# Pooling layer in groups of 1024 tokens, its input units as seven half-block products: a two-layer float32 trunk on one core

## The chip, the core and the metric

The kernel runs on one core of a Trainium2 chip. The core has five engines with a queue of instructions each: TensorE (PE, matrix products, into the banks of PSUM), VectorE (DVE), ScalarE (ACT), GpSimd (POOL) and SyncE (SP, which here issues all DMAs, in order). Each queue runs in its own order, and an instruction waits for semaphores of others. The metric is the device time of one execution in microseconds. Three runs of the kernel before gave 2665.26, 2665.99 and 2666.0 us, median 2665.99.

## What is computed

4096 tokens of width 1024 go through two layers with a norm ahead of each and one at the end, all in float32. The first layer is attention in a window of 128 with a learned sink for each head; the second subtracts each channel from its trailing mean over 2, 4, 8 or 16 tokens, mixes channels in four groups and gates the result.

```python
def attn_layer(h, w_in, sinks, w_out):
    proj = h @ w_in
    q, k, v, z = jnp.split(proj, ...)
    o = swa_with_sinks(q, k, v, sinks)
    return (o * jax.nn.silu(z)) @ w_out

def pool_layer(h, w_in, w_mix, scale, w_out):
    u, z = jnp.split(h @ w_in, [POOL_WIDTH], axis=-1)
    p = multiscale_pool(u)
    m = jnp.einsum('bsgc,gcd->bsgd', p, w_mix).reshape(B, S, POOL_WIDTH) * scale
    return (m * jax.nn.silu(z)) @ w_out

def reference(...):
    for i in range(DEPTH):
        h = rmsnorm(x, norm_g[i])
        y = attn_layer(...) if i % N_MIXERS == 0 else pool_layer(...)
        x = x + y.astype(x.dtype)
    return rmsnorm(x, final_g)
```

## The kernel before

Tokens are columns. They are worked on in 8 groups of 512 (`G`), first all groups through attention (s = 0 to 7), then all through pooling (s = 8 to 15). A **unit** is the product of 256 output channels with 512 tokens over all 1024 inputs: 48 matmuls (`in_piece`, L238). Every float32 operand is split into a high part, rounded to PE's float32r, and a low part that holds the rest (`split_sb`: ACT writes the high part, L121, DVE subtracts for the low part, L122); the three products high x high, high x low, low x high (`PASSES`) are accumulated. That gives 8 chunks of inputs x 2 halves of outputs x 3 passes.

An attention group has units k, v, q (4), z (4) and, for the group before it, four output units; between their matmuls stand 16 softmax items (4 sets of heads x 4 blocks of 128 queries): `it_scores` (scores, masked, exponentials on ACT), 0.9 of a unit later `it_turn` (transposes on PE, then DVE and POOL), 0.8 later `it_pv`. A pooling group has units u (4) and z (4), and four output units of the group before it. The pooling weights for u are first multiplied with the mixing matrices (`prep_load`, `prep_mm`, into `wum` in memory), so that mixing and input projection are one product.

The order of work is a list of events: `at(t, fn, ...)` notes what is to be done at time t, counted in units, with the offsets in the table `T`; the list is sorted by t and run once to build the program, and the framework then puts the instructions on each engine's queue by its own plan. In the last attention group (s = 7) z ends the group; the first pooling group (s = 8) goes u, z, u, then the four output units of s = 7, then the rest. So products of the pooling layer stand ahead of attention's last output units and behind them.

Weights are loaded and split when a unit first uses them (`w_load`, `w_split`), the parts are stored (`wparts`) and loaded again for later groups (`w_again`, 1024 KB at a time, L149, three tiles). The residual stream between the layers goes through memory: `x1` is written by `ev_o` (L456) and read by `xt_load` (L161) and `res_load`. Sums of squares for the norms are made in passing (`square`), summed over channels by a product with ones (`total`), sent through memory to be laid out differently (`rsd`, `rsq`) and broadcast (`spread`, L213). The last output unit is cut in two halves of 256 tokens, so that the end of the first half runs beside the second (`last_piece`, L473; `last_final`, L503).

Of the kernel before, what the change touches and what calls it, by code (L numbers as in the profile page):

```python
# [21 lines left out]
NG = S // G  # L22
NB = G // 128
# [14 lines left out]
         a2=6.8, a3=9.3, ad=0.55, pl=1.3, pm=0.5, pmd=0.5, aturn=0.9, apv=0.8)  # L38
# [7 lines left out]
def trunk_kernel(ctx, tc, xt, ng, w_a_in, sinks, w_a_out, wu_t, wmix, pscale, w_b_z, w_b_out, fg, out):  # L46
# [4 lines left out]
    hp = E(tc.tile_pool(name="hp", bufs=1))  # L51
    wp = E(tc.tile_pool(name="wp", bufs=1))
    sp = E(tc.tile_pool(name="sp", bufs=1))
    psum = E(tc.tile_pool(name="psum", bufs=1, space=PSUM))

    x1 = [dram.tile([4, 128, 2, G], F32, name=f"x1_{g}") for g in range(NG)]
    rsd = [dram.tile([1, G], F32, name=f"rsd_{g}") for g in range(3 * NG)]
# [20 lines left out]
    one8 = const.tile([128, 4, 128], I8, name="one8")  # L78
    nc.gpsimd.memset(one8, 1)
    mask = const.tile([128, 4, 128], I8, name="mask")  # L80
    nc.gpsimd.affine_select(out=mask, in_=one8, pattern=[[0, 4], [1, 128]], compare_op=ALU.is_ge,
                            fill=0.0, base=-1, channel_multiplier=-1)
    ucar = const.tile([128, 4, 2, 16], F32, name="ucar")
    nc.vector.memset(ucar, 0.0)
    cfix = const.tile([128, 4, 16], F32, name="cfix")
    nc.vector.memset(cfix, 1.0)
    for j, w in enumerate(WINDOWS):
        for t in range(w - 1):
            nc.gpsimd.memset(cfix[:, j, t:t + 1], float(w) / (t + 1))

# [12 lines left out]
    pool_tiles = {}  # L103
# [54 lines left out]
    def xt_load(s):  # L158
        for n in range(4):
            t = sp.tile([128, 2, G], F32, tag="xt", bufs=4, name=f"xt{s}_{n}")  # L160
            nc.sync.dma_start(t, xt[s, n] if s < NG else x1[s - NG][n])  # L161
            xts[s, n] = t
# [14 lines left out]
    def rstd(key, near=False):  # L177
# [7 lines left out]
        parts = [sp.tile([128, G], F32R, tag=t, bufs=1, name=f"{t}{key}") for t in ("sr", "sl")]  # L185
# [14 lines left out]
    def spread(key, near=False):  # L200
# [10 lines left out]
        nc.sync.dma_start(rsq[key].rearrange("o (p c) -> (o p) c", c=NB), rs)  # L211
        bc = sp.tile([128, G], F32, tag="bc", bufs=1, name=f"bc{key}")
# [6 lines left out]
    def x_scale(s, k):  # L219
        t = xts[s, k // 2][:, k % 2]  # L220
        nc.vector.scalar_tensor_tensor(t, t, ng_sb[:, s // NG, k:k + 1], bcs[s], op0=ALU.mult, op1=ALU.mult)  # L221
# [182 lines left out]
    us = {}  # L404

    def ev_u(U, s, j):
        ps = acc.pop(U)
        first = s == NG
        u = sp.tile([128, 2, G + 16], F32, tag="q", bufs=2, name=f"u{s}_{j}")
        nc.scalar.copy(u[:, :, 0:16], ucar[:, j])  # L410
        nc.scalar.copy(u[:, :, 16:], ps)  # L411
        nc.scalar.copy(ucar[:, j], u[:, :, G:G + 16])
        if "sums" not in pool_tiles:
            pool_tiles["sums"] = sp.tile([128, 2, 2, G + 16], F32, tag="vm", name="sums")
        tmps = [pool_tiles["sums"][:, i] for i in range(2)]
        w = WINDOWS[j]
        src, step, lo, i = u, 1, 0, 0
        while step < w:
            dst = tmps[i]
            lo += step  # L420
            nc.vector.tensor_add(dst[:, :, lo:], src[:, :, lo:], src[:, :, lo - step:G + 16 - step])
            src, step, i = dst, 2 * step, 1 - i
        if first:
            nc.vector.tensor_mul(src[:, :, 16:32], src[:, :, 16:32], cfix[:, j].unsqueeze(1).to_broadcast([128, 2, 16]))
        p = sp.tile([128, 2, G], F32, tag="o", bufs=2, name=f"p{s}_{j}")
        nc.vector.scalar_tensor_tensor(p, src[:, :, 16:], 1.0 / w, u[:, :, 16:], op0=ALU.mult, op1=ALU.subtract)
        us[s, j] = p

    def gate_b(s, j):
        gate(s, j, us.pop((s, j)))  # L430


    ress = {}
    rslot = [0]

    def res_load(s, n):
        if s < NG:
            t = sp.tile([128, 2, G], F32, tag="res", bufs=2, name=f"res{s}_{n}")
            nc.sync.dma_start(t, xt[s, n])
        else:  # L440
            i = rslot[0] % 5
            rslot[0] += 1
            if "res" not in pool_tiles:
                pool_tiles["res"] = sp.tile([128, 5, 2, G], F32, tag="kt", name="resb")
            t = pool_tiles["res"][:, i]
            nc.sync.dma_start(t, x1[s - NG][n])
        ress[s, n] = t

    def ev_o(U, s, n):
        ps = acc.pop(U)  # L450
        t = ress[s, n]
        if s == 2 * NG - 1 and n == 3:
            return
        nc.vector.tensor_add(t, t, ps)  # L454
        if s < NG:
            nc.sync.dma_start(x1[s][n], t)  # L456
            del ress[s, n]
            return
        square(NG + s, n, t, nc.vector)


    HT = G // 2

    def last_piece(U, i8):
        s, half = 2 * NG - 1, i8 // 4
        cols = slice(HT * half, HT * half + HT)
        if i8 % 4 == 0:
            acc[U] = mm_tile(f"mm{U}_{half}")
        ps = acc[U]
        for k in range(2 * (i8 % 4), 2 * (i8 % 4) + 2):  # L470
            for c in range(2):
# [35 lines left out]
    def final(s):  # L507
        bc = bcs.pop(NG + s)
        for k in range(NK):
            t = ress[s, k // 2][:, k % 2]  # L510
            nc.vector.scalar_tensor_tensor(t, t, fg_sb[:, k:k + 1], bc, op0=ALU.mult, op1=ALU.mult)
            if k % 2:
                nc.sync.dma_start(out[s - NG, k // 2], ress.pop((s, k // 2)))
# [200 lines left out]
```

## Time and profile before

| | |
|---|---|
| median of three runs | 2665.99 us |
| the profiled execution | 2667.01 us, of which the span is 2665.3 |
| mean granted clock of PE | 0.997 of full speed |
| matmuls of units, 128x512, with h (L238) | 6528, 1549.2 us busy |
| matmuls of output units, 128x512, with a (L238) | 3024, 703.3 us busy |
| matmuls of scores (L331) | 1024, 148.6 us busy |
| memory traffic | 487.65 MB read, 92.36 MB written, 218 GB/s over the span |

The profile lists busy time by engine and by group of instructions (line, engine, operation, tiles out<-in, shapes, count; busy us, mean ns of one; idle time of the engine just before them and what ended it). It also gives busy time in any stretch of time, who waited for whom, and instructions in order of time. PE is matmuls, PEld the weight loads beside them. A group's mean is of single durations; matmuls overlap, so their rate is read from start to start.

### The profile page before, as it was taken

How to read it: one execution, taken by the hardware profiler on the slowest of the kernel's cores; microseconds unless marked ns; L12 is line 12 of the kernel's file. 1: busy time of each engine (PE TensorE's matmuls, PEld its weight loads, DVE VectorE, ACT ScalarE, POOL GpSimd, SP SyncE). 2: the span in 40 equal slices, each digit the busy share in tenths (PEclk: the TensorE clock that was granted, in tenths of full speed). 3: DMA queues.
4: the chain of work that ended last, by engine and by line, in shares of the span. 5: the costliest groups of instructions: out<-in, count | busy, mean ns of one | idle time of the engine just before them, and what ended most of it. 6: DMA issues, size and time to landing. Idle time of an engine off the chain costs nothing.

```text
span 2665.3 us, 34728 instructions
## 1 busy us (share of the span) xinstructions
PE 2602.9 (98%) x12732; PEld 2185.8 (82%) x12732; DVE 1611.1 (60%) x2744; ACT 993.4 (37%) x2528; POOL 629.6 (24%) x984
## 2 busy tenths in 40 slices
PE   6999999999999999999999999999999999999998
PEld 5878888888888888888888878888888888888887
DVE  6898667576576675675685674554545454535343
ACT  5566345354354353353462442322222222222111
POOL 1353343343343352352443330000000000000000
PEclk9999999999999999999999999999999999999999
DMA  7855754655555555546546478876767676767564
GB/s 277 292 195 187 267 189 170 213 177 187 195 180 184 194 180 185 198 169 217 182 173 219 163 276 302 290 256 228 256 237 252 230 255 226 261 222 261 195 245 155
DMA packets 109814, 582.29 MB, mean 218 GB/s; under 512 B 18102, under 2 KB 20150, under 8 KB 56396
## 3 DMA queue, kind: packets, MB, share of 16 engines
q1 hardware_dynamic: 109644, 580.07, 61.9%
q8 instruction: 101, 1.65, 0.2%
q14 instruction: 69, 0.57, 0.1%
HBM read 487.65 MB, written 92.36 MB: 218 GB/s over the span
## 4 chain that ended last, share of the span: by engine, by line
issue 42%; PE 40%; DVE 11%; ACT 4%; DMA 2%; POOL 2%; POOLq 0%; SPq 0%; DVEq 0%; ACTq 0%
PE mm L238 29%; PE s L331 3%; PE mm L248 3%; ACT P L346 2%; PE pT L358 2%; PE po L389 1%; DVE m L369 1%; DVE m L365 1%; DVE h L122 1%; POOL rs L204 1%; DVE xt L221 1%; DVE sq L173 1%; DVE mx L342 1%; DVE o L398 1%; DVE q L283 1%
## 5 line engine op out<-in xcount | busy, mean ns | idle before, releaser
L238 PE MATMUL mm<-h,w 128*128 128x512 f32 x6528 | 1549.2, 392 | 7.1 <-DMA w<-wparts 3.8
L238 PEld LDWEIGHTS mm<-h,w 128*128 128x128 f32 x6528 | 1207.1, 188 | 249.8 <-DMA w<-wparts 5.9
L238 PE MATMUL mm<-a,w 128*128 128x512 f32 x3024 | 703.3, 390 | 0.6 <-ACT u L411 0.6
L238 PEld LDWEIGHTS mm<-a,w 128*128 128x128 f32 x3024 | 563.4, 188 | 115.6 <-ACT u L411 1.1
L346 ACT ACTIVATE P<-s,nm 128x128 f32<-128x128 f32 x512 | 181.3, 367 | 266.5 <-DVE nm L343 216.4
L351 POOL TENSOR_TENSOR P<-P,sm 128x512 f32<-128x512 f32 x128 | 141.0, 1101 | 565.3 <-DVE sm L350 355.0
L204 POOL TENSOR_TENSOR rs<-ms,mhalf 128x4 f32<-128x4 f32 x23 | 26.4, 1150 | 1024.4 <-DVE ms L203 947.1
L377 POOL TENSOR_SCALAR_AFFINE_SELECT m<-m 64x512 fp32r<-64x512 f32 x256 | 189.2, 739 | 59.0 <-DVE m L369 55.7
L314 DVE SCALAR_TENSOR_TENSOR sz<-th,mm 128x512 f32<-128x512 f32 x128 | 87.7, 685 | 146.2 <-ACT th L313 144.7
L375 POOL TENSOR_SCALAR_AFFINE_SELECT m<-m 64x256 fp32r<-64x256 f32 x256 | 117.0, 457 | 229.6 <-ACT m L364 221.2
L397 ACT COPY tmp<-po 64x256 f32<-64x256 f32 x256 | 94.1, 368 | 192.4 <-DVE o L398 95.1
L454 DVE TENSOR_TENSOR resb<-resb,mm 128x1024 f32<-128x1024 f32 x31 | 37.9, 1221 | 207.6 <-PE mm L238 207.6
L331 PEld LDWEIGHTS s<-kt,q 128*128 128x128 f32 x1024 | 141.1, 191 | 19.8 <-ACT P L346 4.8
L173 DVE TENSOR_TENSOR sq<-sq,sr 128x512 f32<-128x512 f32 x166 | 118.2, 712 | 64.4 <-ACT sr L172 62.6
L331 PE MATMUL s<-kt,q 128*128 128x256 f32 x1024 | 148.6, 285 | 4.1 <-ACT P L346 2.1
L313 ACT ACTIVATE th<-mm 128x512 f32<-128x512 f32 x128 | 76.6, 599 | 191.3 <-PE mm L238 142.6
L398 DVE TENSOR_TENSOR o<-po,tmp 64x256 f32<-64x256 f32 x256 | 108.0, 422 | 65.9 <-ACT tmp L397 60.5
L379 POOL TENSOR_SCALAR_AFFINE_SELECT m<-m 64x256 fp32r<-64x256 f32 x256 | 138.5, 541 | 13.6
L283 DVE TENSOR_TENSOR q<-mm,q 64x512 fp32r<-64x512 f32 x128 | 88.2, 689 | 61.2 <-ACT q L282 59.5
L337 DVE COPY_PREDICATED s<-mask,s 128x512 f32<-128x512 int8 x124 | 85.7, 691 | 57.8 <-PE s L331 57.0
L221 DVE SCALAR_TENSOR_TENSOR xt<-xt,ng_sb,bc 128x512 f32<-128x512 f32 x128 | 91.5, 761 | 41.2 <-DMA bc<-rsq 39.1
L172 ACT ACTIVATE sr<-resb 128x512 f32<-128x512 f32 x54 | 34.0, 629 | 216.2 <-DVE resb L454 198.4
(108 smaller groups left out, 2511.7 us busy)
## 6 DMA issues: line engine op xcount, KB each, us to landing
w<-wparts SPq DMA_DIRECT2D x364, 1024.0 KB, 4.9
wparts<-w SPq DMA_DIRECT2D x52, 1024.0 KB, 4.8
xt<-in_xt SPq DMA_DIRECT2D x32, 512.0 KB, 4.4
res<-in_xt SPq DMA_DIRECT2D x32, 512.0 KB, 3.4
x<-res SPq DMA_DIRECT2D x32, 512.0 KB, 5.9
xt<-x SPq DMA_DIRECT2D x32, 512.0 KB, 5.3
resb<-x SPq DMA_DIRECT2D x32, 512.0 KB, 5.2
out<-resb SPq DMA_DIRECT2D x28, 512.0 KB, 2.6
```

Source lines behind the costliest of these rows:

```text
L173: engine.tensor_add(sums[key], sums[key], q)
L221: nc.vector.scalar_tensor_tensor(t, t, ng_sb[:, s // NG, k:k + 1], bcs[s], op0=ALU.mult, op1=ALU.mult)
L238: nc.tensor.matmul(ps[:, c], w[:, wl, k % 4, 128 * c:128 * c + 128], rhs(k, hl), start=(k == 0 and i == 0), stop=(k == NK - 1 and i == 2))
L283: nc.vector.tensor_sub(q[64 - r:128 - r, h], src, f32(q[r:r + 64, h]))
L331: nc.tensor.matmul(ps[:, h], qs[s, j][:, h, 128 * b:128 * b + 128], kt[:, j, hl, 128 * b:128 * b + 256], start=(hl == 0), stop=(hl == 1))
L346: nc.scalar.activation(P[:, h], sc[:, h], AF.Exp, bias=nm[:, h:h + 1], scale=SCALE, accum_out=sm[:, h:h + 1])
L351: nc.gpsimd.tensor_mul(P, P, sm.unsqueeze(2).to_broadcast([128, 4, 128]))
L375: nc.gpsimd.affine_select(out=m2[own, :, cols], in_=f32(m1[own, 0, :, cols]), compare_op=ALU.is_ge, fill=0.0, **keep)
L377: nc.gpsimd.affine_select(out=mv, in_=f32(mv), compare_op=ALU.is_ge, fill=0.0, **drop)
L379: nc.gpsimd.affine_select(out=mv, in_=f32(mv), compare_op=ALU.is_ge, fill=0.0, **keep)
L397: nc.scalar.copy(tmp[d:d + 64], pv[e:e + 64, :, r])
L398: nc.vector.tensor_add(o[d:d + 64, :, 128 * b:128 * b + 128], pv[d:d + 64, :, r], tmp[d:d + 64])
```

## The change

**Groups and products.** Pooling now runs over four groups of 1024 tokens, two blocks of 512. An input unit (256 outputs x 1024 tokens over 1024 inputs) is seen as a product of 2x2 half-blocks: outputs in halves of 128, inputs in halves of 512, tokens in two blocks. The product of 2x2 blocks is formed with seven products in place of eight (`product`, L571), each of 12 matmuls, from sums of blocks (Winograd's form). The left factors, sums of weight blocks, are made once in attention groups 2 to 7: `seven_load` and `seven`, 24 calls, four to a group, with four POOL sums, seven splits and seven stores each for u and z, and four splits for output weights. The right factors, sums of blocks of tokens (T1 to T4 beside B11, B21, B22), are made for each group by POOL (`factor_sum`) and split by ACT and DVE (`factor`, L117 and L118). Seven products go into three PSUM banks X, Y, Z; as X is accumulated further for other results, its contents are copied out in between by ACT (`snapshot`), three times a unit. A unit's product 3 is done within the next unit.

**Order.** A pooling group runs its eight input units and then its own four output units (`o_pair`, L620, 96 matmuls each, four banks); pooling of one group and output of another no longer alternate. The pooling stage has its own pools of SBUF and PSUM, opened when attention's are closed (`open_pools`). The last attention group has another order of units and softmax offsets (`e0` to `e3`), and attention's last output units are followed by the pooling stage alone. The squares for the first pooling group's norm are made in attention (`x1_square`). The final norm of a group is applied in pieces during the next group (`final_piece`), from a copy in memory (`x2`); the last output unit is cut in pieces of 512, 256 and 256 tokens (`last_pair`, L741; `last_scale`, L783).

The core of the diff:

```diff
+NP = NG // 2
...
+        a11, a12, a21, a22 = v[:, 0, 0], v[:, 1, 0], v[:, 0, 1], v[:, 1, 1]
+        S = wp.tile([128, 4, 2, 128], F32, tag="wraw", bufs=2, name=f"sum7_{key[0]}{key[1]}_{hf}")
+        g = nc.gpsimd
+        g.tensor_add(S[:, 0], a21, a22)
+        g.tensor_sub(S[:, 1], S[:, 0], a11)
+        g.tensor_sub(S[:, 2], a11, a21)
+        g.tensor_sub(S[:, 3], a12, S[:, 1])
+        for i, m in enumerate((a11, a12, S[:, 3], a22, S[:, 0], S[:, 1], S[:, 2])):
+            t = sp.tile([128, 2, 2, 128], F32R, tag="sl", bufs=2, name=f"part7_{key[0]}{key[1]}_{hf}_{i}")
+            if i == 3:
+                nc.scalar.mul(t[:, 0], m, -1.0)
+                nc.vector.scalar_tensor_tensor(t[:, 1], m, -1.0, f32(t[:, 0]), op0=ALU.mult, op1=ALU.subtract)
+            else:
+                split_sb(t[:, 0], t[:, 1], m)
+            nc.sync.dma_start(wseven[key][i][:, hf], f32(t))
...
+    RIGHT = {1: "B11", 2: "B21", 3: "B22", 4: "T4", 5: "T1", 6: "T2", 7: "T3"}
...
+    def factor_sum(g, name, p):
+        ph = (g, "in")
+        b11, b12, b21, b22 = (quarter(ph, p, t, k) for k in range(2) for t in range(2))
+        sub = nc.gpsimd.tensor_sub
+        if name == "T1":
+            sub(b11, b12, b11)
+        elif name == "T3":
+            sub(b12, b22, b12)
+        elif name == "T2":
+            tmp2[p] = bt([128, G], "t2", 4, f"t2_{g}_{p}")
+            sub(tmp2[p], b22, b11)
+        else:
+            sub(tmp2[p], tmp2[p], b21)
...
+    def factor(ph, name, p):
+        src = quarter(ph, p, *PLACE[name]) if name in PLACE else tmp2[p]
+        t = bt([128, 2, G], "set", 28, f"set_{ph[0]}{ph[1]}_{name}_{p}", F32R)
+        split_sb(t[:, 0], t[:, 1], src)
+        sets[ph, name, p] = t
...
+    def w7_load(u, i):
+        src = wout[u[2]][i] if u[1] == "o" else wseven[u[1], u[2]][i - 1]
+        t = bt([128] + list(src.shape[1:]), "w7", 5, f"w7_{u[0][0]}{u[1]}{u[2]}_{i}", F32R)
+        nc.sync.dma_start(f32(t), src)
...
+    def product(u, i):
+        bank = {1: "X", 6: "X", 7: "X", 4: "X", 2: "Y", 5: "Z", 3: "Z"}[i]
+        first = i in (1, 2, 5)
+        if first:
+            banks[u, bank] = bpsum(bank, 2, f"{bank}_{u[0][0]}{u[1]}{u[2]}")
+        ps, w = banks[u, bank], w7.pop((u, i))
+        for a, p in enumerate(PAIRS):
+            t = sets[u[0], RIGHT[i], p]
+            for b, (wl, hl) in enumerate(PASSES):
+                nc.tensor.matmul(ps, w[:, p // 2, wl, p % 2], t[:, hl], start=(first and a == 0 and b == 0),
+                                 stop=(a == 3 and b == 2), skip_group_check=True)
...
+    def snapshot(u, n, t):
+        nc.scalar.copy(blk(u, n, t), banks[u, "X"])
...
+    def h_load(g, p):
+        r = raws[(g, "in"), p] = bt([128, 2, 2, G], "raw", 4, f"xr{g}_{p}")
+        for t in range(2):
+            nc.sync.dma_start(r[:, t], x1[2 * g + t][p])
...
+    def h_scale(g, p):
+        for k in range(2):
+            r = raws[(g, "in"), p][:, :, k]
+            nc.vector.scalar_tensor_tensor(r, r, ng_sb[:, 1, 2 * p + k:2 * p + k + 1], bbc["h", g], op0=ALU.mult, op1=ALU.mult)
...
+        if 2 <= s < NG:
+            for i in range(4):
+                k, hf = sevens[4 * (s - 2) + i]
+                t = base + 1.0 + 3.2 * i
+                at(t, seven_load, k, sources[k[0]][k[1]], hf)
+                at(t + 0.8, seven, k, hf)
...
+    at(base, open_pools)
...
+            order = [1, 6, 5, 7, 2, 4] if prev is None and g else [1, 2, 5, 6, 7, 4] if prev is None else [1, 3, 6, 5, 7, 2, 4]
```

**What moves on the engines.** SP's queue where attention ends, before the change (`x1_7` is the residual stream of the last attention group, `wum` and `in_w_b_z` are pooling weights):

```order
L456 DMA x1_7_79<-res7_2_15594 128x1024
L145 DMA wparts_115_0_15755<-w115_0_15752 128x2048
L136 DMA wraw116_0_15757<-wum_2_130 128x1024
L145 DMA wparts_115_1_15798<-w115_1_15795 128x2048
L136 DMA wraw116_1_15806<-wum_2_130 128x1024
L456 DMA x1_7_79<-res7_3_15651 128x1024
```

Weights of the next pooling units stand ahead of the last store of attention's results. The same place with the change (`w7_...` are left factors, `bch0` the norm's broadcast, `xr0_p` the activations of the first 1024 tokens, in four pairs of chunks p):

```order
L413 DMA x1_7_79<-res7_2_16134 128x1024
L413 DMA x1_7_79<-res7_3_16191 128x1024
L559 DMA w7_0u3_1_16367<-w7_u3_0_13078 128x1024
L559 DMA w7_0u3_2_16369<-w7_u3_1_13079 128x1024
L559 DMA w7_0u3_5_16371<-w7_u3_4_13082 128x1024
L559 DMA w7_0u3_6_16373<-w7_u3_5_13083 128x1024
L559 DMA w7_0u3_7_16375<-w7_u3_6_13084 128x1024
L703 DMA bch0_16377<-rsq_8_116 128x512
L703 DMA bch0_16377<-rsq_9_117 128x512
L708 DMA xr0_3_16380<-x1_0_72 128x1024
L708 DMA xr0_3_16380<-x1_1_73 128x1024
L708 DMA xr0_2_16383<-x1_0_72 128x1024
```

All loads of the pooling layer now stand behind that store, the weights first. PE's queue at the same place, before (`mm110` is the second u unit of the first pooling group, `mm111` the first output unit of attention's last group):

```order
L238 MATMUL mm110_15479<-h8_6_15163,w110_1_15438 128x512 x6
L238 MATMUL mm110_15479<-h8_7_15187,w110_1_15438 128x512 x6
L193 MATMUL ms9_15942<-sr9_15895,ones_r_144 128x512
L193 MATMUL ms9_15942<-sl9_15896,ones_r_144 128x512
L238 MATMUL mm111_15567<-a0_7_14509,w111_0_15486 128x512 x12
L238 MATMUL mm111_15567<-a1_7_14751,w111_0_15486 128x512 x12
```

And with the change (the last output unit of attention, then the first input unit `0u3`; `set_0in_B11_p` is a split right factor):

```order
L236 MATMUL mm111_16276<-a3_7_16104,w111_1_16254 128x512 x12
L571 MATMUL X_0u3_16482<-set_0in_B11_3_16394,w7_0u3_1_16367 128x512 x3
L571 MATMUL X_0u3_16482<-set_0in_B11_2_16400,w7_0u3_1_16367 128x512 x3
L571 MATMUL X_0u3_16482<-set_0in_B11_1_16406,w7_0u3_1_16367 128x512 x3
L571 MATMUL X_0u3_16482<-set_0in_B11_0_16412,w7_0u3_1_16367 128x512
L571 MATMUL Y_0u3_16498<-set_0in_B21_3_16416,w7_0u3_2_16369 128x512
```

The first pooling product comes directly behind attention's last matmul. ACT's queue in that first input unit (COPY rows of L588 are snapshots of bank X, CAST rows the high parts of factors); before the change there were no snapshots and no factors:

```order
L117 CAST set_0in_T3_0_16476<-xr0_0_16389 128x512
L588 COPY ct_0u3_16480<-X_0u3_16482 128x512
L117 CAST set_0in_T4_3_16529<-t2_0_3_16431 128x512
L117 CAST set_0in_T4_2_16532<-t2_0_2_16436 128x512
L117 CAST set_0in_T4_1_16535<-t2_0_1_16441 128x512
L117 CAST set_0in_T4_0_16538<-t2_0_0_16446 128x512
L117 CAST set_0in_B22_3_16555<-xr0_3_16380 128x512
L117 CAST set_0in_B22_2_16558<-xr0_2_16383 128x512
L117 CAST set_0in_B22_1_16561<-xr0_1_16386 128x512
L117 CAST set_0in_B22_0_16564<-xr0_0_16389 128x512
L588 COPY ct_0u3_16480<-X_0u3_16482 128x512
```

The unit's second snapshot stands behind the casts of T4 and B22.

531 lines of the change are left out of this document (387 added, 144 removed).

## The prediction

> **What bounds the kernel now.** I read the totals and the clock slices on the page first, then busy time in stretches of 200 us, then PE's waits, then the order in time where attention hands over to pooling.
>
> ```profile
> span 2665.3 us, 34728 instructions
> PE 2602.9 (98%) x12732; PEld 2185.8 (82%) x12732; DVE 1611.1 (60%) x2744; ACT 993.4 (37%) x2528; POOL 629.6 (24%) x984
> PEclk9999999999999999999999999999999999999999
> ```
>
> PE is busy 98% of the span at full clock. A busy PE alone proves little, so the stretches and the waits come next (columns: stretch, length, then busy us and instructions of PE, PEld, DVE, ACT, POOL, granted clock, DMA share, GB/s).
>
> ```profile
> 100.00:200.00 100.00, 95.14 (x485) 78.13 (x484) 89.10 (x168) 58.63 (x171) 51.67 (x77) 1.00 0.66 227
> 600.00:800.00 200.00, 197.32 (x1019) 167.19 (x1019) 135.36 (x273) 91.65 (x276) 81.11 (x127) 1.00 0.52 188
> 1800.00:2000.00 200.00, 200.00 (x884) 165.62 (x883) 91.26 (x109) 44.96 (x75) 2.39 (x2) 1.00 0.68 239
> PE mm L238 <- DMA w<-wparts: 3.8, 5, 1.3
> ```
>
> The last line is all that PE waited for between 1600 and 2620 us. Attention runs to about 1600 us, pooling from there. In both stages the matmul stream is the limit, and in pooling almost nothing interrupts it. The rate and the hand-over stand in PE's order in time:
>
> ```profile
> 1583.98 43.83 PE L238 MATMUL mm<-a,w 128*128 128x512 f32 x192 [0.65 <-ACT u L411]
> 1627.65 65.44 PE L238 MATMUL mm<-h,w 128*128 128x512 f32 x288
> 1692.93 27.36 PE L238 MATMUL mm<-a,w 128*128 128x512 f32 x120
> ```
>
> From start to start, (1692.93 - 1627.65)/288 = 0.2267 us for one matmul of 512 columns; 12 of them take 2.72 us. The hand-over costs 0.65 us today, because u and z products of the first pooling group stand on both sides of attention's last output units.
>
> **The change, part by part.** Sums are against the profiled run: 2667.01 us with a span of 2665.3, so 1.7 us lie around it; the median of the three runs is 1.0 lower. I apply the sum of changes to the median, 2665.99.
>
> *Matmuls, -87.0.* Pooling had 12 units x 8 groups x 48 = 4608 matmuls of 512 columns. Now four groups have 8 input units x 7 products x 12 = 672 and 4 output units x 96 = 384, together 4224 (the last output unit is in narrower pieces in both). 384 x 0.2267 = 87.0 us, and PE is what sets the end there, so all of it counts. Attention keeps its matmuls.
>
> *The hand-over, +44.* This is the large cost. The order on SP puts every load of the pooling layer behind the store of attention's last result. Nothing of PE's work is left to cover them, as attention's output units are now its last products. Rows for the walk (groups, then DMA issues with KB and us to landing, then two stretches of DMA):
>
> ```profile
> L122 DVE TENSOR_TENSOR h<-xt,h 128x512 fp32r<-128x512 f32 x128 | 90.4, 720 | 0.9
> L319 DVE SCALAR_TENSOR_TENSOR sz<-o,sz 128x1024 f32<-128x1024 f32 x32 | 39.1, 1221 | 0.5
> L454 DVE TENSOR_TENSOR res<-res,mm 128x1024 f32<-128x1024 f32 x32 | 39.1, 1222 | 48.5 <-PE mm L238 48.2
> L351 POOL TENSOR_TENSOR P<-P,sm 128x512 f32<-128x512 f32 x128 | 141.0, 1101 | 565.3 <-DVE sm L350 355.0 <-ACT m L364 81.0 <-PE mm L238 52.9
> L121 ACT CAST h<-xt 128x512 fp32r<-128x512 f32 x128 | 79.3, 620 | 54.1 <-PE mm L238 43.0 <-DVE xt L221 7.1 <-DVE h L122 1.5
> out<-resb SPq DMA_DIRECT2D x8, 256.0 KB, 2.5
> 204.00:206.00 2.00, 2.00 (x11) 1.61 (x10) 1.43 (x5) 1.95 (x8) 0.90 (x1) 1.00 0.96 385
> ```
>
> Clock zero is attention's last matmul. The residual add takes 1.2 us, the store's issue some 0.5. Ahead of the first activations' arrival lie the store (0.5 MiB), five weight tiles (2.5), two broadcasts (0.5) and those activations (1.0): 4.7 MB at 385 GB/s is 12.3 us. A 256 KB store takes 2.5 us to land, of which 0.7 is transfer, so 1.8 us is fixed. The first pair is there at about 15.9, the other three 2.7 apart.
>
> Then come scalings (8 at 1.22 on DVE) and splits into high part (ACT, 0.62) and low part (DVE, 0.72), while POOL makes the sums: 16 subtractions, priced like its 128x512 tensor_tensor at 1.10. If DVE and POOL overlapped, DVE alone would set the pace. These rows say they do not:
>
> ```profile
> 721.49 0.89 POOL L375 TENSOR_SCALAR_AFFINE_SELECT m<-m 64x256 fp32r<-64x256 f32 x2 [2.90 <-ACT m L364]
> 737.16 1.22 DVE L319 SCALAR_TENSOR_TENSOR sz<-o,sz 128x1024 f32<-128x1024 f32 x1
> 737.46 1.67 POOL L375 TENSOR_SCALAR_AFFINE_SELECT m<-m 64x256 fp32r<-64x256 f32 x2 [4.74 <-ACT m L364]
> ```
>
> The same two POOL selects take 0.89 us, but 1.67 when DVE is inside an operation with two SBUF operands: 737.46 + 1.67 - 0.89 = 738.24, about when DVE's operation ends (738.38). The scalings, the low parts and POOL's subtractions are all of that kind, so I add their times. (The Trainium skill, SBUF — State Buffer, section "Who interferes with whom", says the same: DVE's second SBUF input comes through the read interface that GpSimd uses, and the loser blocks for the whole instruction; this row agrees. Without that rule the sum would take the 29 us below for 45.)
>
> To POOL's last sum: 8 x 1.22 + 16 low parts x 0.72 + 16 x 1.10 = 38.9, so 54.8. ACT then casts that sum and, ahead of the second snapshot of bank X in its queue, four B22 factors: 5 x 0.62, and 0.62 for the snapshot, 58.5. Product 7 waits for it (61.2), product 4 for the next snapshot (with four other matmuls, about 64.9), product 3 ends at 67.6. PE has by then done 8 products and four matmuls, 22.7 us of work: **45 us idle**, 44 more than today. With DVE alone, POOL's last sum is at 15.9 + 21.3 + 1.1 = 38.3, and idle about 29. Worst, with 300 GB/s and both engines fully in series, 52.
>
> *Attention's added work, +13.* 24 calls of `seven` cut the pooling weights into parts: 112 subtractions of 256 columns and 32 of 512 on DVE, and 16 squares are made there too. By the nearest rows (0.42 for 256 columns, 0.72) that is some 80 us of DVE in groups 2 to 7, about 1200 us: its share goes from 0.68 to 0.75. In the two attention stretches above PE lost 1.3% at a DVE share of 0.68 and 4.9% at 0.89; in proportion, 0.067 more share costs 1.1% of 1200, 13 us. That includes the tighter last group. Below, nothing, if the spaces hide it; above, 4.9% throughout: 41.
>
> ```profile
> L478 DVE TENSOR_TENSOR resb<-resb,mm 128x256 f32<-128x256 f32 x4 | 1.5, 418 | 3.0 <-PE mm L473 3.0
> ```
>
> *Seams between pooling groups, +9.* At three seams the snapshot of a group's first product stands on ACT behind the squares of the old group's last output: after PE's last output matmul come an add (0.72), a square (0.62), POOL's add (1.10, behind two low parts, 1.4), a cast and the snapshot (0.62 each), 5.1 us, against 2.72 for the first product. So PE idles about 2.4 us, and then runs cold:
>
> ```profile
> 212.00:214.00 2.00, 1.23 (x6) 0.66 (x4) 2.00 (x5) 0.17 (x1) 0.00 (x0) 1.00 0.00 0
> 214.00:216.00 2.00, 0.79 (x2) 0.51 (x3) 1.19 (x4) 2.00 (x11) 0.00 (x0) 0.84 0.83 254
> 216.00:218.00 2.00, 2.00 (x10) 2.00 (x10) 0.98 (x3) 1.95 (x4) 1.04 (x1) 0.50 0.66 274
> 218.00:220.00 2.00, 2.00 (x10) 1.60 (x9) 1.85 (x4) 0.83 (x3) 0.00 (x0) 0.81 0.00 0
> 215.21 1.11 PE L238 MATMUL mm<-h,w 128*128 128x512 f32 x2 [1.98 <-DVE sz L314]
> ```
>
> A gap of 1.98 us left the granted clock at 0.84, 0.50 and 0.81 for 2 us each: 2 x (0.16 + 0.50 + 0.19) = 1.7 us lost. Three times 4.1 is 12.3, less the 3.8 us of weight waits, whose loads now have five tiles in flight. (The Trainium skill, TensorE: Matmul & The Clock Gate, "Part 1", wants an idle window of about 3.4 us before the clock halves; the row halves it after 1.98. By the page the seams would cost 3 x 2.4 - 3.8 = 3.) From 0 to 25 us: snapshots inside a unit have a whole product, 2.72 us, to be taken.
>
> *The tail, +4.*
>
> ```profile
> 2650.32 1.67 PE L473 MATMUL mm<-a,w 128*128 128x256 f32 x12
> 2658.74 3.22 DVE L503 SCALAR_TENSOR_TENSOR resb<-resb,fg_sb,bc 128x256 f32<-128x256 f32 x8 [2.09 <-PE bc L500]
> ```
>
> Today the last scaling begins 6.75 us after the last matmul (2651.99). Now the eight 512-wide scalings of the first 512 tokens, 8 x 0.72 = 5.8 us, stand in DVE's queue ahead of the last result, some 3 us of them past the last matmul, and the chain behind waits: about 4 us (0 to 6).
>
> *Memory traffic, 0.* A product takes one 512 KB tile per 2.72 us, 193 GB/s, today's rate for units; output units need half of that. With pieces of the last norm some 270 GB/s, under the 385 above. If that cover goes, each late tile costs what today's do, 0.8 us.
>
> Sum: -87.0 + 44 + 13 + 9 + 4 = -17; 2665.99 - 17 = **2649**.
>
> **Rivals.** *DVE and POOL overlap after all* (operands from PSUM do not block, and the sums might slip in between): hand-over 29 instead of 45, **2633**. For it: in the attention stretches DVE and POOL together are busy longer than the stretch; against it: most of DVE's operations there read PSUM, and the row above.
>
> *Slower: the parts' stores hold ACT and DVE.* `seven` has two slots for parts, so ACT's cast of a part waits in its queue until the store of two parts earlier has landed, with softmax work queued behind it.
>
> ```profile
> x<-res SPq DMA_DIRECT2D x32, 512.0 KB, 5.9
> PE pT L358 <- DVE m L369: 17.2, 11, 2.2
> ```
>
> A store in attention takes up to 5.9 us to land, an idle one 2.5. If each of the 24 calls made PE wait as long as its longest wait on DVE now, 2.2 us, that is 53 us, 40 above my 13: **2689**. It decides from (17 + 13)/24 = 1.25 us a call. Against it: the order spreads a call's parts among other rows on ACT, and the transposes stand 0.9 of a unit, about 10 us, after their scores.
>
> *Snapshots late inside the units*: 96 on ACT and each a possible gap. At 0.25 us each, 24 us: **2673**. Against it: ACT was 22% busy in pooling, and a product stands between.
>
> *The products are not as fast*: 12 matmuls now go to one bank in a row, where a unit's today change banks after 3. Each ns more is 4.2 us, so 4 ns would eat the gain: **2666**. No row shows such a price.
>
> **How the numbers follow.** Forecast as walked, 0.55: **2649**, with its terms' own spread from 2636 to 2665. Overlap or a cheaper hand-over, 0.25: 2608 to 2636. Slower by stores, 0.10; late snapshots, 0.07; slower products, 0.03: 2660 to 2700. The range takes in the first two and half of the rest: 2614 to 2676. A measurement here tells 0.2%, 5.3 us, from no change: faster means under 2660.7. From the forecast 0.48 lies below it and 0.07 within; with the second case, and 0.02 of the rest, faster is 0.75; within 0.12; slower 0.13.
>
> **What would show it.** PE's product rows should start 0.227 apart, with 4224 of them. Between attention's last matmul and pooling's steady run, PE should show about 45 us without work; if DVE's low parts there stay at 0.7 and POOL's subtractions at 1.1 while both are busy, the lock is wrong and 29 should stand. POOL's sums longer than 1.5 us would show it right. Waits of PE on DVE and ACT in attention should grow by 13 us in all. The three seams should show gaps of about 2 us with the clock at 0.50 behind. I am wrong if SP's loads start before attention's last store, or if PE's waits in groups 2 to 7 exceed 30 us.

## Result and the profile after

The changed kernel takes **2732.82 us** (median of 4 runs, 2728.4 to 2737.86) against 2665.99 (2665.26 to 2666.42): ratio 1.0252, 95% interval 1.0228 to 1.0275. It is 67 us slower, where 2649 was forecast in a range of 2614 to 2676. The profiled execution has a span of 2727.0 us, 61.7 more than before. First the totals and the clock slices of the page of after, then busy time in the two longer stretches shown of before, with the same columns:

```profile
span 2727.0 us, 35659 instructions
PE 2551.1 (94%) x12362; PEld 2124.1 (78%) x12362; DVE 1795.9 (66%) x2958; ACT 1076.8 (39%) x2774; POOL 871.2 (32%) x1164
PEclk9999999999999999999999997999899989998999
```

```profile
600.00:800.00 200.00, 195.63 (x996) 164.07 (x996) 147.86 (x299) 103.27 (x306) 88.31 (x130) 0.99 0.68 239
1800.00:2000.00 200.00, 176.54 (x767) 144.55 (x766) 128.71 (x139) 60.70 (x108) 54.11 (x34) 0.95 0.64 217
```

PE was busy 98% of the span and is busy 94%. The clock slices were 9 throughout and now have four dips: one where attention hands over, three later at equal distances. Attention lost a little, and the pooling stretch, which had no idle microsecond, has 23 us in 200. What PE waited for from 1600 us to the end (us in total, times, longest):

```profile
PE ms L684 <- ACT sro L117: 58.6, 3, 20.0
PE X_0u L571 <- ACT set_0in_B L117: 23.0, 4, 19.1
PE X_0u L571 <- DVE set_0in_B L118: 7.1, 4, 2.4
```

The hand-over is there as walked (X_0u: group 0). New is the first line: three waits of nearly 20 us in the norm total of the old group (`b_total`), one for each seam between pooling groups. PE's order in time gives the size of each term (start, us, then what; rows from attention's last matmuls to the last product):

```profile
1614.83 6.06 PE L236 MATMUL mm<-a,w 128*128 128x512 f32 x26
...
1905.10 2.88 PE L571 MATMUL X_1u<-set_1in_B,w_1u 128*128 128x512 f32 x12
1927.62 0.80 PE L684 MATMUL ms<-sro,ones_r 128*128 128x512 f32 x1 [19.64 <-ACT sro L117]
...
2056.26 2.88 PE L571 MATMUL X_1u<-set_1in_T,w_1u 128*128 128x512 f32 x12
2058.99 2.88 PE L571 MATMUL Y_1u<-set_1in_B,w_1u 128*128 128x512 f32 x12
...
2174.20 2.88 PE L571 MATMUL X_2u<-set_2in_B,w_2u 128*128 128x512 f32 x12
...
2441.27 2.88 PE L571 MATMUL X_3u<-set_3in_B,w_3u 128*128 128x512 f32 x12
...
2709.01 1.68 PE L741 MATMUL last<-set_3out_B,w_3o 128*128 128x256 f32 x12
```

A product starts 2.73 us after the one before it (2056.26, 2058.99): the cadence of 0.2267 us a matmul holds. A group has 672 + 384 matmuls and up to 8 of norm totals, 1064 x 0.2267 = 241.2 us. From start to start it takes 269.1 and 267.1, and 269.4 from the last start to the last matmul, where about 242 would do: **81 us lost in the three stretches that hold the seams**. Some 7 of them lie elsewhere: PE's short waits for snapshots inside the units (1.5 us at most). From attention's end (1620.9) to 1905.1 it is 284.2, where 240.3 would do (1060 matmuls): 43.9 for the hand-over. In before attention's last matmul ended at 1627.65 with 144 pooling matmuls done ahead of it by the order, so 32.6 us of that was pooling's; 1595.0 against 1620.9 is 26 for attention. From the last product to the end it was 13.3 and is 16.3. The division between two terms is this execution's: in nine later runs that left attention as it is, attention ended up to 10 us earlier, and in eight that left the hand-over as it is, that stretch was up to 6 us longer.

| term (us) | forecast | measured |
|---|---|---|
| matmuls | -87.0 | -87.0 |
| hand-over | +44 | +43 |
| attention | +13 | +26 |
| seams, less the weight waits of 3.8 | +9 | +77 |
| tail | +4 | +3 |
| sum | -17 | +62 (61.7 between the two spans) |

Now the first seam. DVE (1874 to 1927 us) and POOL (to 1928) from the first scaling of the next group on, grouped (count, busy us, mean ns, idle before), then PE, DVE and ACT in order of time where PE stands still:

```profile
L718 DVE SCALAR_TENSOR_TENSOR xr<-xr,ng_sb,bch 128x1024 f32<-128x1024 f32 x8 | 15.1, 1924 | 10.7 <-issue 10.7
L118 DVE TENSOR_TENSOR set_1in_B<-xr,set_1in_B 128x512 fp32r<-128x512 f32 x11 | 13.3, 1229 | 0.6 <-ACT set_1in_B L117 0.6
L118 DVE TENSOR_TENSOR set_1in_T<-xr,set_1in_T 128x512 fp32r<-128x512 f32 x8 | 13.0, 1687 | 0.0
```

```profile
L535 POOL TENSOR_TENSOR xr<-xr 128x512 f32<-128x512 f32 x4 | 8.5, 2137 | 10.6 <-DVE set_1in_B L118 10.6
L540 POOL TENSOR_TENSOR t<-xr 128x512 f32<-128x512 f32 x4 | 6.9, 1734 | 0.0
```

```profile
1903.74 1.52 PE L620 MATMUL pt_0o<-set_0out_B,w_0o 128*128 128x512 f32 x6
1914.88 3.55 DVE L118 TENSOR_TENSOR set_1in_B<-xr,set_1in_B 128x512 fp32r<-128x512 f32 x4
1918.36 2.48 DVE L118 TENSOR_TENSOR set_1in_T<-t,set_1in_T 128x512 fp32r<-128x512 f32 x4
1920.77 0.67 DVE L626 TENSOR_TENSOR ct_0o<-ct_0o,X_0o 128x512 f32<-128x512 f32 x1
1925.66 0.68 DVE L626 TENSOR_TENSOR ct_0o<-ct_0o,pt_0o 128x512 f32<-128x512 f32 x1
1926.97 0.60 ACT L117 CAST sro<-sqo 128x512 fp32r<-128x512 f32 x1
```

PE finished the old group's last product at 1905.3. DVE adds it to the residual only at 1925.7, in its four parts from 1920.8 on: its queue holds the next group's scalings and low parts ahead of that add, with the old group's other adds 52 us of work (the burst, below) begun at 1874.0, 31 us before the seam. A scaling takes 1.92 us in the mean instead of 1.22, and a low part of T1 and T3 1.69 (the others 1.0 to 1.2) instead of 0.72. POOL's 16 subtractions run beside them, at means of 1.7 to 2.1 us; run 4 shows that they are the reason. Squares, sums and the total wait for that add, and PE waits for the total.

### The profile page after: what moved, and what is told of

Its sections match the earlier page's. It is cut to its first block, busy times and chain, and to the rows that moved or that the text cites. A ratio compares the mean times of both kernels' runs of the same rounds, so it can differ in the third digit from the quotient of the medians.

```text
span 2727.0 us, 35659 instructions
## 1 busy us (share of the span) xinstructions
PE 2551.1 (94%) x12362; PEld 2124.1 (78%) x12362; DVE 1795.9 (66%) x2958; ACT 1076.8 (39%) x2774; POOL 871.2 (32%) x1164
## 5 line engine op out<-in xcount | busy, mean ns | idle before, releaser
L236 PE MATMUL mm<-h,w 128*128 128x512 f32 x3456 | 852.4, 396 | 2.7 <-DVE sz L312 1.9
L236 PEld LDWEIGHTS mm<-h,w 128*128 128x128 f32 x3456 | 634.3, 190 | 124.5 <-DVE sz L312 2.4
L236 PE MATMUL mm<-a,w 128*128 128x512 f32 x1536 | 366.7, 392 | 0.0
L236 PEld LDWEIGHTS mm<-a,w 128*128 128x128 f32 x1536 | 283.5, 188 | 56.1
L329 PEld LDWEIGHTS s<-kt,q 128*128 128x128 f32 x1024 | 140.4, 191 | 33.9 <-ACT P L344 16.3
L367 DVE TENSOR_TENSOR m<-pT,m 64x256 fp32r<-64x256 f32 x256 | 107.9, 422 | 7.8
L363 DVE TENSOR_TENSOR m<-pT,m 128x512 fp32r<-128x512 f32 x128 | 88.0, 688 | 25.3 <-ACT m L362 22.2
L344 ACT ACTIVATION_READ_ACCUMULATOR P<-s,nm 128x1 f32 x512 | 104.2, 204 | 0.0
L280 ACT CAST q<-mm 64x512 fp32r<-64x512 f32 x128 | 74.3, 581 | 75.5 <-DVE q L281 51.1
L362 ACT CAST m<-pT 128x512 fp32r<-128x512 f32 x128 | 75.4, 589 | 58.8 <-PE pT L356 28.4
L246 PE MATMUL mm<-w,h 128*128 128x256 f32 x768 | 97.8, 286 | 0.0
```

Source lines behind the costliest of these rows:

```text
L236: nc.tensor.matmul(ps[:, c], w[:, wl, k % 4, 128 * c:128 * c + 128], rhs(k, hl), start=(k == 0 and i == 0), stop=(k == NK - 1 and i == 2))
L246: nc.tensor.matmul(ps[:, b], hts[s, k][:, hl, 128 * b:128 * b + 128], wtiles[U, k // 4][:, wl, k % 4], start=(k == 0 and i == 0), stop=(k ...
L329: nc.tensor.matmul(ps[:, h], qs[s, j][:, h, 128 * b:128 * b + 128], kt[:, j, hl, 128 * b:128 * b + 256], start=(hl == 0), stop=(hl == 1))
L344: nc.scalar.activation(P[:, h], sc[:, h], AF.Exp, bias=nm[:, h:h + 1], scale=SCALE, accum_out=sm[:, h:h + 1])
L367: nc.vector.tensor_sub(m2[other, :, cols], pv[own, :, cols], f32(m1[own, 0, :, cols]))
```

## Experiments

Times below are medians of 4 to 11 runs beside runs of the kernel before (2663.3 to 2665.2 us). "Stretches" are the four between the points above: hand-over, and three seams (284.2, 269.1, 267.1, 269.4 in after). T3, B21, T4 and B22 are the factors that products 7, 2, 4 and 3 use. Attention was left as it is in nine of the runs, and yet in these and the changed kernel it ended between 1610.5 and 1620.9 us; what is gained there counts only beyond that.

**1. The total at the head of PE's queue, or DVE's backlog?**

```diff
-                at(pos + 3.0, b_total, ("o", g - 1), t)
+                at(pos + 23.0, b_total, ("o", g - 1), t)
```

> Edit: the norm total of the old pooling group (and what follows from it) is put 20 us later in the order, behind the first unit's products; nothing else. Theory A (DVE's queue is 20 us late at the seam, because the next group's scalings and low parts stand ahead of the last output's adds): the second product still needs the snapshot of the first, which stands on ACT behind the squares of the same adds, so PE's three waits only change their name, from the total (58.6 us) to the X bank behind ct (50 to 60 us); 2720 to 2735 us. Theory B (the total's matmul at the head of PE's queue blocks products that are ready): the 58.6 us and the cold clock behind them go, about 2670 us.

2746.57 us. PE's waits in the first seam's stretch, 1900 to 1980 us:

```profile
PE X_1u L571 <- ACT ct_1u L588: 12.4, 2, 12.1
PE Z_1u L571 <- ACT set_1in_T L117: 6.5, 1, 6.5
```

The waits have other names and together nearly the same length (18.9 against 19.6 us). The total was the first to wait, not the cause. The run is also 14 us slower than the changed kernel, above both forecasts; why was not looked into.

**2. Factors later in the source.**

```diff
-            at(op + 71.0 + 0.1 * i, factor, ph, "T3", p)
+            at(pos + 0.2 + 0.1 * i, factor, ph, "T3", p)
```

(B21, T4 and B22 in the same way.)

> Edit: at the three seams the factors T3, B21, T4 and B22 of the next group (16 casts, 16 low parts) are ordered behind the last output's adds instead of ahead of them. Theory A: these low parts took some 15 us of DVE ahead of the last adds (1908.8 to 1926), so PE's waits on the total fall from 19.5 to about 5 us each, some of it comes back as waits of product 7 on T3; 2680 to 2700 us. Theory B: the total is still the second thing in PE's queue and still waits for a chain of its own; 2725 to 2735 us.

2733.57 us, the waits 57.8. This tells nothing of the theory, since the edit did not reach the queue: DVE's order still has the 12 low parts of T3, B21 and T4 ahead of the last output's first add, as without the edit. The framework orders the queue by its own plan, and the place in the event list is not the place in the queue.

**3. The norm earlier.**

```diff
-            at(op + 10.0 + 6.0 * i, h_square, g + 1, p)
+            at(op + 12.0 + 1.5 * i, h_square, g + 1, p)
-            at(op + 34.0, b_total, ("h", g + 1), t)
+            at(op + 22.0, b_total, ("h", g + 1), t)
```

> Edit: the squares of the next group's norm close together (op+12 to 16.5 instead of op+10 to 28) and its total at op+22 instead of op+34; nothing else. Theory A with the norm's chain as its start (total on PE at 1854, four transfers, first scaling at 1874, 31 us before the output products end): scalings start 10 to 12 us earlier, each wait falls from 19.5 to about 8 us, 2690 to 2700 us. If DVE's 52 us of work were not what counts: 2725 to 2735 us.

2714.9 us; the three waits fell from 58.6 to 35.2, the stretches to 262.9, 263.2 and 260.5. The burst now starts 43 us before the seam, at 1860.3, and each wait is 8 us shorter. The direction is right; the waits fell by two thirds of what was expected, and the time by 18 us, about half.

**4. The subtractions on DVE.**

```diff
-        sub = nc.gpsimd.tensor_sub
+        sub = nc.vector.tensor_sub
```

> Edit: the 64 subtractions of the right factors go from POOL to DVE; nothing else. Lock (an operation of DVE with two SBUF operands and one of POOL exclude each other): 16 x (1.10 - 0.68) = 6.7 us less at the hand-over and at each of the three seams, DVE's scalings go back from 2.27 to 1.22 us and its low parts from 1.7 to 0.68; about 2706 us. No lock: DVE alone gets 16 x 0.68 = 10.9 us more at four places, about 2775 us.

**2684.24 us**, 49 less with one word changed, and with more work on the engine that is late. DVE's groups at the same seam, 1860 to 1903 us:

```profile
L718 DVE SCALAR_TENSOR_TENSOR xr<-xr,ng_sb,bch 128x1024 f32<-128x1024 f32 x8 | 10.2, 1282 | 9.5 <-DMA bch<-rsq 9.5
L118 DVE TENSOR_TENSOR set_1in_T<-xr,set_1in_T 128x512 fp32r<-128x512 f32 x8 | 5.1, 682 | 0.0
L535 DVE TENSOR_TENSOR xr<-xr 128x512 f32<-128x512 f32 x4 | 2.8, 689 | 0.0
```

The scaling is back at 1.28 and the low part of T1 and T3 at 0.68; a subtraction takes 0.69 here, and took POOL 1.7 to 2.1. The burst lasts 42 us instead of 52. The hand-over stretch went to 273.9, the seams to 255.7, 256.5 and 258.8: 10 to 13 us at each of four places, where 6.7 was expected from POOL's undisturbed 1.10. (This agrees with the rule of the Trainium skill, SBUF — State Buffer, "Who interferes with whom", that the two engines lock each other out of a shared port.)

**5. The last adds forced ahead of the late factors.**

```diff
+        with tc.issue_after(add.ins), tc.issue_after(square.ins):
+            factor(ph, name, p)     # T3, B21, T4, B22; add, square: the last of the old group
```

> Edit: as in the run before with T3, B21, T4 and B22 later, but with the order on DVE and ACT forced: their low parts and casts are issued behind the last output unit's last add and square at each of the three seams. Theory A (the last adds stand late in DVE's queue): the adds come some 13 us earlier, PE's waits on the total fall from 19.5 to below 6 us each; product 7 and those behind it then wait 3 to 8 us for factors that come later; 2690 to 2705 us. If the adds' place in DVE's queue is not the cause: 2725 to 2735 us, with the waits as they were.

2715.75 us; stretches 289.1, 263.9, 262.8, 261.8. Now the adds come where PE ends (DVE, order in time; the group's first product started at 1908.6):

```profile
1911.36 0.68 DVE L626 TENSOR_TENSOR ct_0o<-ct_0o,X_0o 128x512 f32<-128x512 f32 x1
1913.15 0.67 DVE L626 TENSOR_TENSOR ct_0o<-ct_0o,pt_0o 128x512 f32<-128x512 f32 x1
1921.50 3.61 DVE L118 TENSOR_TENSOR set_1in_T<-xr,set_1in_T 128x512 fp32r<-128x512 f32 x4 [7.67 <-ACT set_1in_T L117]
```

The last add is at 1913.2 instead of 1925.7, 4.5 us after the group's first start instead of 20.6. PE's waits of 19.5 us became 7, but DVE then stands idle for 7.7 us: the casts of T3 are behind the squares on ACT, and the squares have two slots that POOL's sums free one by one. The three stretches fell by only 4 to 8 us each; the rest went into new waits, and the run stayed 11 us above the expected range.

**6. Norm earlier and subtractions on DVE together** (edits 3 and 4).

> Edit: the norm's squares and total 12 us earlier and the 64 subtractions on DVE, together. Theory A with the lock: the burst (42 us of DVE without POOL) now starts 43 instead of 32 us before the seam and is over when the output products end, so the three waits go but for 1 to 2 us each; the stretches between group starts fall from 256 to about 245 us; 2684 - 33 = about 2651 us. If the two edits gain the same microseconds: 2675 to 2685 us.

2682.22 us, against 2684 with the subtractions alone. The stretches are 275.5, 255.1, 254.2, 259.5: nothing beyond edit 4. The last adds do come sooner (2.3 to 7.2 us behind the group's first start, 7.6 to 9.4 with edit 4 alone), but PE's order changed too: the total now stands behind product 1 and no longer behind product 6, and PE waits some 6 us for it at each seam (18.2 in three). The two edits gained the same microseconds, as the second line of the expectation has it.

**7. Loads at the hand-over: activations ahead of weights.**

```diff
-        at(uses[n - 6] + 0.1 if n > 5 else base, w7_load, u, i)
+        at(uses[n - 6] + 0.1 if n > 5 else base + 0.05, w7_load, u, i)
-                at(t, h_load, 0, p)
+                at(base + 0.02, h_load, 0, p)
```

> Edit: at the hand-over the norm's broadcast and the pooling activations are loaded ahead of the first five weight tiles (2.5 MiB) instead of behind them; nothing else. If the hand-over starts with the wait for the first activations, as walked: 2.5 MiB at 385 GB/s is 6.8 us less, stretch from attention's last matmul to the second group's start 284 to 277 us, 2726 us in all. If the chain behind the arrival hides it (later pairs, DVE and POOL): below 2 us.

2727.73 us, hand-over stretch 283.4. The first scaling came 10.3 us after attention's last matmul instead of 17.1, as computed, and the microseconds went elsewhere (PE's waits, 1600 to 1700 us):

```profile
PE X_0u L571 <- DMA w_0u<-w_u: 19.3, 1, 19.3
PE X_0u L571 <- ACT ct_0u L588: 8.8, 1, 8.8
```

The first weight tile is now late, and the second snapshot of bank X stands on ACT behind the casts of T4.

**8. Attention without the cutting of the weights.**

```diff
-                split_sb(t[:, 0], t[:, 1], raw[:, c])
-                nc.sync.dma_start(wout[key[1]][2 * hf + c // 2][:, :, c % 2], f32(t))
+                nc.sync.dma_start(wout[key[1]][2 * hf + c // 2][:, :, c % 2], raw[:, 0:2])
```

(u and z in the same way, their sums too.)

> Edit: the casts, subtractions and sums that cut the pooling weights into parts during attention are left out (the pooling weights are then not the right ones); their loads and as many stores of the same size stay. If the arithmetic on DVE, ACT and POOL is what made attention's groups 3.7 to 9.1 us longer (191 to 195-200 us): they go back to 191 to 192, 2733 - 25 = about 2708 us. If the transfers (3.8 MiB a group more) or their place in SP's queue do it: no change of the groups, 2728 to 2738 us.

2715.51 us; attention ends at 1598.9, 22 us earlier. Stretch 200 to 1400 us, of before, after and this run:

```profile
200.00:1400.00 1200.00, 1182.03 (x6154) 1004.85 (x6153) 817.57 (x1623) 552.40 (x1628) 476.02 (x736) 1.00 0.55 191
```

```profile
200.00:1400.00 1200.00, 1168.48 (x5975) 984.89 (x5974) 871.43 (x1737) 591.12 (x1748) 525.25 (x784) 0.99 0.66 230
```

```profile
200.00:1400.00 1200.00, 1179.11 (x6130) 1000.29 (x6129) 818.20 (x1621) 553.35 (x1628) 475.05 (x735) 1.00 0.66 233
```

The memory traffic of the third row is that of the second (233 and 230 GB/s), its engines' load that of the first. So the arithmetic costs the time, not the transfers. PE is busy 13.6 us less in after than in before, and the clock is 0.99 instead of 1.00 (0.9915 and 0.9986 from the clock records): another 8.5 us. Over the ten executions with the same attention the two vary: 9 to 15 us of busy time, 2 to 10 us of clock.

**9. The seams and the hand-over mended.** Edits 1, 3, 4 and 5, and besides:

```diff
-        b_square(("o", u[0][0]), u[2] == 3 and n == 0, b, t, nc.gpsimd)
+        square = b_square(("o", u[0][0]), u[2] == 3 and n == 0, b, t, nc.vector)
-        at(uses[n - 6] + 0.1 if n > 5 else base, w7_load, u, i)
+        at(uses[n - 6] + 0.1 if n > 5 else base + (0.025, 0.035, 0.05, 0.051, 0.052)[n - 1], w7_load, u, i)
-                at(t, h_load, 0, p)
+                at(base + (0.02, 0.03, 0.04, 0.045)[i], h_load, 0, p)
+        with tc.issue_after(snaps[(ph, "u", 3), 0, 1].ins):
+            factor(ph, name, p)
```

The last two lines put T4 and B22 of the first group behind the second snapshot; the loads put two weight tiles between those of the activations.

> Edit: together the norm 12 us earlier, the 64 subtractions and the sums of the old group's squares on DVE, the last adds forced ahead of T3, B21, T4 and B22, the norm total of the old group 20 us later; at the hand-over the activations' loads ahead of four of the five weight tiles, and T4 and B22 of the first group behind the second snapshot. Theory A: what is left at a seam is only a few short waits, the stretches between group starts go from 267-269 us (after) and 254-259 us (norm and subtractions) to 244-248 us, the hand-over stretch from 284 to about 266; with attention at 1610-1620: about 2645 us. If another wait takes their place (late factors, snapshots): 252 us and more a stretch, 2670 us.

**2657.37 us** (10 runs, 2648.5 to 2664.2), ratio 0.9978 with a 95% interval of 0.9966 to 0.9991: 75 us faster than the changed kernel, and some 0.2% faster than the kernel before; 12 us more than was expected. Stretches 269.5, 248.4, 247.6, 249.7. DVE at its first seam (first product of the group at 1884.58):

```profile
1880.70 0.69 DVE L632 TENSOR_TENSOR ct_0o<-ct_0o,X_0o 128x512 f32<-128x512 f32 x1 [2.57 <-PE X_0o L626]
1884.79 0.69 DVE L632 TENSOR_TENSOR ct_0o<-ct_0o,pt_0o 128x512 f32<-128x512 f32 x1
```

DVE now waits for PE ahead of the last adds and makes the last of them at the seam. The three stretches lose some 7 us each (248.4 - 241.2), 21 together instead of 81. PE waits nowhere for the total, and 12.7 of the 21 are waits for snapshots inside the units. In the profiled execution attention ended at 1615.1; with 20 us for attention, 29 for the hand-over, 21 - 4 for the seams and 3 for the tail, less 87, the sum is -18, and its span of 2646.5 is 18.8 below that of before. It was the fastest of the ten, 9 us under their median.

**10. The hand-over's two edits alone** (the last six lines of the diff above).

> Edit: only the two edits at the hand-over (order of the loads, T4 and B22 of the first group behind the second snapshot on ACT). In the run with the loads first PE lost 19.3 us to the first weight tile and 8.8 us to a snapshot behind the casts of T4. If these two ate what the earlier activations gave: stretch 284 to 272-276 us, about 2720 us. If DVE and POOL in series set the end of the hand-over alone: 282 to 285 us, no change.

2723.44 us; stretch 276.6. Both losses of run 7 are gone, and 8 us with them.

**11. The sums of half blocks on DVE.**

```diff
-        g = nc.gpsimd
+        g = nc.vector
```

> Edit: the 64 sums of half blocks with which the weights are cut in attention (POOL, 128x256) go to DVE; nothing else. The arithmetic of the cutting costs about 22 us of attention. If it is POOL's operations that hold DVE: attention 1610 us or less (10 us of the 22 gained). If DVE's load is what counts (share 0.72, then 64 x 0.42 = 27 us more): attention 1625 to 1630 us.

2733.56 us, attention's end at 1620.1: neither. Beyond the scatter it makes no difference which of the two engines does these 64 sums. The stretch of 200 to 1400 us again, of this run:

```profile
200.00:1400.00 1200.00, 1164.93 (x5990) 980.91 (x5989) 897.50 (x1807) 592.92 (x1752) 479.60 (x725) 1.00 0.66 231
```

DVE is busy 26 us more than in after and POOL 46 us less. So DVE's load alone does not set what attention loses.

**12 and 13. Load, or ACT waiting for stores?** ACT in after waited between 450 and 1250 us for the parts' stores, as the rival had it:

```profile
ACT part_z L117 <- DMA w_z<-part_z: 53.9, 19, 6.5
...
ACT part_u L117 <- DMA w_u<-part_u: 40.5, 17, 6.3
...
ACT part_o L117 <- DMA wo<-part_o: 17.8, 10, 6.1
```

In the first run the parts are computed but slices of the uncut weights stored, so that no cast waits for a store; in the second each cast is issued behind what was traced on ACT before it:

```diff
-            nc.sync.dma_start(wseven[key][i][:, hf], f32(t))
+            nc.sync.dma_start(wseven[key][i][:, hf], raw[:, 0:2].rearrange("p a (k d) -> p a k d", k=2))
...
+            with tc.issue_after(last_act()):
+                split_sb(t[:, 0], t[:, 1], m)
```

> Edit: the parts are computed as in the changed kernel, but the stores send slices of the uncut weights in their place (the pooling weights are then not the right ones), so that no cast waits for a store of a part before it; as many stores of the same size. If the waits of ACT for the parts' stores are the price: attention ends at about 1600 us as without the cutting, 2710 us in all. If the load of the casts and subtractions is the price: it ends at 1615 to 1621 us, 2728 us.

> Edit: the parts of a call are 0.3 of a unit apart in the order and each cast is issued on ACT behind what was traced there before it; nothing else. If ACT's waits for the stores are the price: most stores have landed by then, attention ends 8 to 15 us earlier (1605 to 1612 us). If it is load: 1617 to 1622 us.

2733.49 and 2730.36 us; attention ends at 1614.1 and 1617.0. In neither run are the three waits among ACT's seven longest. Both ends lie within the scatter of 1610.5 to 1620.9, the one without arithmetic (1598.9) 12 us outside. 112 us of waits of ACT in 800 cost at most a few microseconds; the load costs the rest. How these 12 to 22 us divide between ACT and DVE was not tried.

**14. Edits 9 and 13 together.**

> Edit: the seams and the hand-over mended as in e9, and the parts apart as in e13. Whatever e13 gains in attention is gained here too: 2657 less 0 to 15 us, 2642 to 2657 us; at 2649 or below all terms of the forecast but the matmuls would be accounted for.

2661.19 us, ratio 0.9987 (0.9979 to 0.9996); attention ends at 1620.5, stretches 270.1, 249.4, 250.8, 251.0. This lies above the expected range: nothing beyond run 9, as run 13 had nothing to give.

## Why the prediction was wrong

- **Matmuls**: right. 2.73 us a product, and 12 matmuls in a row to one bank cost nothing.
- **Hand-over**: right in size and cause. 43.9 us lost against 45; first scaling 17.1 us after attention's last matmul against 15.9; POOL and DVE in series, as run 4 confirms. POOL's last sum (T4) ended 54.0 us after attention, against 54.8, and product 7, which needs the second snapshot, started at 57.3, against 58.5:

```profile
1668.15 6.75 POOL L542 TENSOR_TENSOR t<-t,xr 128x512 f32<-128x512 f32 x4 [3.64 <-DVE set_0in_T L118]
1678.17 3.01 PE L571 MATMUL X_0u<-set_0in_T,w_0u 128*128 128x512 f32 x12 [2.69 <-ACT ct_0u L588]
```

  Loads that came 6.8 us earlier gained nothing by themselves (run 7) and 8 us with two weight tiles put between them and a snapshot moved (run 10): other waits stand close behind there.
- **Seams: the step that failed.** The prediction walked from PE's last output product through "an add (0.72), a square (0.62), POOL's add (1.10, behind two low parts, 1.4)" to 5.1 us, and so took DVE to be free for that add, with no more of the next group's work than two low parts ahead of POOL. It had made out in the step on the hand-over that scalings, low parts and subtractions are 39 us in series to POOL's last sum, and did not ask when the same work is done for the next groups. It starts when the norm is spread (1874.0), 31 us before the seam, and lasts 52. The backlog of 20 us stood in DVE's queue ahead of the adds, as DVE's rows in order of time show. Shown by runs 1 (not the total), 4 (POOL's subtractions beside it make the burst long) and 5 (the adds' place in the queue), and by 9, where all of it together takes 60 of the 81 us away.
- **Cold clock at the seams**: right in kind, and small. Stretches of 2 us at the first seam (PE's busy us first, the clock third from the end):

```profile
1926.00:1928.00 2.00, 0.38 (x1) 0.38 (x2) 2.00 (x3) 1.14 (x2) 1.73 (x2) 0.50 0.23 88
1928.00:1930.00 2.00, 1.09 (x3) 0.37 (x3) 1.70 (x2) 1.10 (x2) 0.55 (x1) 0.50 1.05 356
1930.00:1932.00 2.00, 2.00 (x5) 1.58 (x6) 0.69 (x1) 0.57 (x1) 0.00 (x0) 0.50 0.95 309
1932.00:1934.00 2.00, 2.00 (x8) 1.60 (x7) 0.00 (x0) 0.00 (x0) 0.00 (x0) 0.80 0.12 45
```

  PE was busy 3.5 us at 0.50 and 2.0 at 0.80: 3.5 x 0.5 + 2 x 0.2 = 2.1 us lost, against 1.7 forecast behind a gap a tenth as long.
- **Attention**: right in kind, the added arithmetic (run 8), and half in size. 13 was read off PE's idle share alone, and 13.6 us of PE's busy time went between 200 and 1400 us; the lower clock was left out, 8.5 us more there. That the loss follows DVE's share, as the proportion had it, is not shown: run 11 raised that share by 26 us of 1200 and attention ended no later. (The 32 subtractions for the output weights have 256 columns, not 512; all 144 took 69 us of DVE.) The rival of the stores had its waits (112 us of ACT), but not the price: runs 12 and 13. The 5.9 us of its row is a median, not the longest.
- **Tail**: 3 against 4.

Of the rivals on the slower side, attention's stores cost little, and late snapshots inside the units some 7 us of the 24 named (12.7 in run 9, where they are most of what is left). The real place, the factors of the next group in DVE's queue ahead of the old group's results, was not among the rivals.

## What to carry to other kernels

Work that is walked out once, at the start of a stage, is to be walked again at every later place where the same instructions stand, with the time from when its input is there to when its output is due: here 52 us of work had 31. Ahead of a result that a product waits for, read what stands in the queue of the engine that makes it, and force the order if need be, since a later time in the source may change nothing. An operation moved from POOL to DVE can make DVE faster, if DVE works on SBUF beside it.

## What the hardware showed beyond that

- DVE and POOL at work on SBUF together lock each other out, and both pay: DVE's scalings 1.92 instead of 1.28 us, its low parts of T1 and T3 1.69 instead of 0.68, POOL's subtractions 1.7 to 2.1 instead of the 1.10 of its 128x512 sums in attention. 64 subtractions off POOL gave 49 us.
- After an idle gap of 19.6 us PE lost about as much to the cold clock (2 us) as after one of 1.98 us in the prediction's rows: between these two, what a gap costs in clock did not grow with its length.
- With the weights cut beside it, attention ended anywhere between 1610.5 and 1620.9 us with the same instructions; what sets this was not found.
